# Cross-attention's output projection in one fixed order with sums grown from the seventh product's, tiles transposed in pairs, and the norm row on partition 96

## Chip, cores and metric

The kernel runs on one core of one Trainium2 chip. The metric is the device time of one execution in microseconds; the median of three runs of the kernel before is 856.6 us (856.55 to 857.37).

## The reference

One layer of an encoder on a residual stream x of 512 tokens by 1024 columns, in float32: a token mixer (HGRN2 and mLSTM heads in both directions), a cross-attention to 256 memory tokens in four heads of 256 columns, and a squared-ReLU MLP of width 4096, each behind an RMSNorm, and a last RMSNorm. The change touches the norm at the start and this part:

```python
def cross_attention(xn, memn, w_q, w_kv, w_o):
    q = (xn @ w_q).reshape(b, s, XATTN_HEADS, XATTN_HEAD_DIM)
    k, v = jnp.split(memn @ w_kv, 2, axis=-1)
    scores = jnp.einsum('bqhd,bkhd->bhqk', q, k).astype(jnp.float32) * (XATTN_HEAD_DIM ** -0.5)
    p = jax.nn.softmax(scores, axis=-1).astype(v.dtype)
    o = jnp.einsum('bhqk,bkhd->bqhd', p, v).reshape(b, s, D_MODEL)
    return o @ w_o

x = x + cross_attention(rmsnorm(x, norm_xattn[l]), rmsnorm(mem, norm_mem[l]), ...)
x = x + squared_relu_mlp(rmsnorm(x, norm_mlp[l]), w_up[l], w_down[l])
```

## The kernel before

**Number format and weights.** Every float32 operand is split in a high part (ScalarE, a copy to fp32r, line 254) and a low part (VectorE, a subtraction, line 255); a product is three matmuls, high by high, high by low, low by high (`mm3`, lines 258 to 260). The weights come in 512 KB blocks of 128 x 1024 in the order of use through SP's queue into three buffers (`load`, line 233); the split parts have three buffers each (`wh`, `wl`), so a block's split waits until TensorE has used the block three places ahead of it. `split` and `weights` make these splits ahead of their use, under high priority.

**Order of instructions.** A scheduler orders each engine's instructions by priority and program order and by what it thinks is ready; every engine then runs its own list strictly in order. In a `manual_schedule` block the listed engines keep program order. Before, TensorE's is the program's order in the first norm and from the loop over the four MLP blocks on, and the scheduler's in between. `behind(a, b)` ties a behind b on their engine.

**Start.** Six small matmuls on a tile of ones keep TensorE running (line 157). The norm's gain row is fetched into row 0 of a tile that VectorE has set to zero (lines 148 and 149, two halves), and a matmul by ones spreads it over all partitions (`spread`, line 161). For each of four token tiles: a sum of squares on ScalarE (`x_stat`, line 327), a power on GpSimd (line 196), scaling on VectorE (`x_scale`, line 332), four transposes (line 337), the split, and the first projection's products. The constants, with the identity for the transposes, come by ScalarE's queue (line 150).

**Cross-attention.** For each head the query projection (`proj_d`) is followed by a chain in three parts that `tick` advances one at a time: scores, softmax and scaling (lines 960 to 970); transposes (line 977) and their split; the product with the values and the sums and differences that the next step takes (lines 1011 to 1013). The chain of head 3 is still open when the output projection begins.

**Output projection.** `by_blocks` does it by a scheme of seven products, P1 to P7, of half-size blocks instead of eight. Each product has two halves g; each half has 24/2 = 12 matmuls of 512 columns for two token tiles u. `JOBS[-1]` gives the order P1, P7, P2, P5, P6, P3, P4. P1, P2 and P3 take plain weight blocks; the others take sums of blocks that are built by GpSimd's accumulating DMAs (line 1053): `sum_loads` loads T3 = (0,1)+(1,1) for P7 and U = (0,1)+(0,0) for P5 during the query projections. When P5's split has read U, block (1,1) is added to it for P6, and when P6's split has read that, (1,0) for P4. `ahead` makes the splits of three jobs under high priority. `finished` adds a product to the residual tiles `xr` (`add_out`, line 1169) once or twice. With a tile's last addition its sum of squares follows (line 906), and, some products later (`turn_whole`), its four transposes (`transp`, line 920), each of whose 128-column blocks ScalarE and VectorE split (lines 925 and 926) into x3T, the MLP's input. The tiles of the last product, P4, are transposed inside `first_two`, which runs the first two products of the MLP and then the transposes of the row of norms (line 1197). GpSimd then starts building the MLP's own sums.

Of the kernel before, what the change touches and what calls it, by code (L numbers as in the profile page):

```python
# [10 lines left out]
F32 = mybir.dt.float32  # L11
# [7 lines left out]
P = 128  # L19
# [61 lines left out]
def trunk(ctx: ExitStack, tc: tile.TileContext, x, mem, wpk, vec, cst, lmask, rmask, rows, out):  # L81
# [55 lines left out]
    def behind(a, b):  # L137

        tc.add_manual_dep(a.ins, b.ins.name, mybir.DependencyInfo(mybir.DependencyClass.NoSync, mybir.DependencyReason.DATA),
                          reason="order of an engine")  # L140

    def load_x(t):
        nc.sync.dma_start(out=xtile[t], in_=x[t * P:t * P + P, :])

    load_x(0)
    for g in range(2):
        z = slice(g * 512, g * 512 + 512)
        v.memset(grow1[:, z], 0.0)
        behind(nh_made, nc.scalar.dma_start(out=grow1[0:1, z], in_=rows[0:1, z]))
    nc.scalar.dma_start(out=cs, in_=cst[:, 0:NC1])  # L150
    gmix = [smb(), smb()]
    idle = mmb()

    def keep_busy(n):

        for _ in range(n):
            pe.matmul(idle[:, 0:P], lhsT=ones[:, 0:P], rhs=ones[:, 0:P], start=True, stop=True)

    def spread(g):

        pe.matmul(gmix[g], lhsT=ones[:, 0:P], rhs=grow1[:, g * 512:g * 512 + 512], start=True, stop=True)

    with tc.manual_schedule(engines={mybir.EngineType.PE}):
        keep_busy(6)
        spread(0)
        keep_busy(3)

    def small_setup():
        lmf = A4()
# [66 lines left out]
    def split(i):  # L236
        if i >= NSTREAM or i in hl_tiles:
            return
        load(i)
        s = st_tiles[i]  # L240
        hi, lo = T("wh", 1024, 3, F32R), T("wl", 1024, 3, F32R)
        split_out(hi, lo, s)
        hl_tiles[i] = (hi, lo)

    def weights(key):
        i = SIDX[key]
# [5 lines left out]

    def split_out(dst_hi, dst_lo, src):
        sc.activation(dst_hi, src, AF.Copy)  # L254
        v.tensor_tensor(out=dst_lo, in0=src, in1=dst_hi.bitcast(F32), op=ALU.subtract)  # L255

    def mm3(ps, ah, al, bh, bl, first, last):
        pe.matmul(ps, lhsT=ah, rhs=bh, start=first, stop=False)  # L258
# [66 lines left out]
    def x_stat(t):  # L325
        ss = tiny(1)
        sc.activation(junk, xtile[t], AF.Square, accum_out=ss)
        rx[t], _ = rstd_of(ss, 1, D)
# [26 lines left out]
    with tc.high_priority(), tc.manual_schedule(engines={ET.PE, ET.DVE, ET.Activation}):  # L355
        x_stat(0)
        x_scale(0, 0)
        x_turn(0, 0)
        spread(1)
        split(0)  # L360
        x_stat(1)
        x_split(0, 0)
        part_v(0, 0)
        x_scale(1, 0)
        x_turn(1, 0)
        split(1)
# [524 lines left out]
    xr = {}  # L891
# [142 lines left out]
    def block(f, g, kh, c):  # L1034
        return SIDX["t", "down" if f >= 0 else "xo", max(f, 0) * 8 + 2 * g + 4 * kh, 512 * c]
# [15 lines left out]
    def add_block(dst, idx, accumulate=True):  # L1051
        kw = dict(accum_op=ALU.add) if accumulate else {}
        return gp.dma_start(out=dst, in_=wpk[idx], **kw)  # L1053

    PLAIN = {"P1": (0, 0), "P2": (1, 0), "P3": (1, 1)}
    SUMS = {f: {"P6": "T2" if f >= 0 else "U", "P5": "U", "P7": "T3", "P4": "T2" if f >= 0 else "U"} for f in range(-1, 4)}

    def job(f, n):

        if n >= len(JOBS[f]):  # L1060
            if f < 3:
                split(SIDX["d", "up", 0, 1024 * (f + 1)] + n - len(JOBS[f]))
            return None
        p, g = JOBS[f][n]
        if p in PLAIN:
# [12 lines left out]
        return jobs_hl[f, n]  # L1078
# [78 lines left out]

    def heads_in(p, g):

        if (p, g) in (("P1", 0), ("P7", 0), ("P7", 1)):  # L1160
            tick()
        while p == "P2" and len(sta_o[2 * g + 1]) < 7:
            tick()
        if (p, g) == ("P5", 0):
            drain()

    def add_out(t, c, ps, sign, last):
        z = xr[t, c]
        v.tensor_tensor(out=z, in0=z, in1=ps, op=ALU.add if sign > 0 else ALU.subtract)
        if last:  # L1170
            stats(st2, t, c)
            whole.append([1 if c else 4, t, c])

    whole = []
# [12 lines left out]
    drain()  # L1187
    x3 = xk(x3T)
# [40 lines left out]

    def first_two():  # L1230

        w = [weights(("d", "up", 0, P * 4 * j)) for j in range(2)]
        two = [mmb(), mmb()]
        transp((x3T, V_MLP), *whole.pop(0)[1:])
        for half in (4, 0):
            for j in range(2):
                for k in range(half, half + 4):
                    z = slice(k * P, k * P + P)
                    mm3(two[j], w[j][0][:, z], w[j][1][:, z], x3[k][0], x3[k][1], k == 4, k == 3)
                    if whole and k == 5:  # L1240
                        transp((x3T, V_MLP), *whole.pop(0)[1:])
        rms_row()
        return two

    ctx.enter_context(tc.manual_schedule(engines={mybir.EngineType.PE}))
    for f in range(4):

        sta = []
# [134 lines left out]
```

## Time and profile before

| | |
|---|---|
| median of three runs | 856.6 us |
| the profiled execution | 856.94 us, its span 855.2 us |
| granted TensorE clock | 0.997 |
| TensorE busy, 0 to 12 us | 9.25 us |
| TensorE busy, 470 to 520 us, in tens of us | 8.76, 10.00, 8.44, 8.83, 8.49 |
| TensorE busy, 540 to 800 us | 60.00 of 60, 100.00 of 100, 100.00 of 100 |
| VectorE busy, 470 to 520 us, in tens of us | 8.07, 9.62, 6.63, 8.82, 9.21 |

The profile records one execution. A row names line, engine, operation and the tile written, with the tiles read behind the arrow; PE is TensorE, PEld its weight loads, DVE VectorE, ACT ScalarE, POOL GpSimd, SP the queue that most loads go through. `L920 ... x4` groups four neighbours in time. Idle time stands in brackets with what ended it. TensorE's ends are modelled, so the distance between two starts is the measure of a matmul.

### The profile page before, as it was taken

Reading aid. Unit: us, or ns where it says so; the run is one execution under the profiler, and the core shown is the slowest. Engines: PE = TensorE matmul, PEld = TensorE weight load, DVE = VectorE, ACT = ScalarE, POOL = GpSimd, SP = SyncE. Lnnn points to the kernel's source line nnn. Section 1 sums busy time; section 2 is a strip of 40 time slices with the busy share of each in tenths; the row PEclk is TensorE's granted clock in tenths of the full one; section 3 lists DMA queues with packets and bytes.
Section 4 is the critical chain, followed back from the end, with each engine's and each line's share of the span. In section 5 each row is a group of like instructions: output and inputs, shape, how many; then the busy total and the mean of one; then the engine's idle time right before and its main releaser. Section 6 shows DMA issues by size and latency. Waiting matters only on the chain.

```text
span 855.2 us, 11759 instructions
## 1 busy us (share of the span) xinstructions
PE 836.6 (98%) x4432; PEld 689.5 (81%) x4432; DVE 591.0 (69%) x1042; ACT 437.0 (51%) x795; POOL 76.8 (9%) x126
## 2 busy tenths in 40 slices
PE   8999999999999999999999989999999999999995
PEld 6788888887977987887888767888888888888884
DVE  5568874599368977555567886776667656866675
ACT  5246454444578485454455475553454334435544
POOL 1000000100010000100000004103101210221001
PEclk9999999999999999999999999999999999999998
DMA  7332223122242332542251357969935992698332
GB/s 267 115 130 80 69 81 136 42 98 78 71 128 73 109 130 91 180 108 98 75 149 50 83 115 242 265 166 236 287 109 126 272 265 99 169 277 217 114 60 99
DMA packets 34124, 118.86 MB, mean 139 GB/s; under 512 B 3922, under 2 KB 4050, under 8 KB 34068
## 3 DMA queue, kind: packets, MB, share of 16 engines
q1 hardware_dynamic: 22832, 77.80, 26.5%
q0 software_dynamic: 10944, 39.85, 21.0%
q8 instruction: 35, 0.57, 0.3%
q10 hardware_dynamic: 292, 0.47, 0.2%
q14 instruction: 21, 0.17, 0.1%
HBM read 116.00 MB, written 2.10 MB: 138 GB/s over the span
## 4 chain that ended last, share of the span: by engine, by line
PE 86%; issue 6%; DVE 3%; DMA 2%; ACT 2%; POOL 1%; POOLq 0%; ACTq 0%; DVEq 0%
PE mm L258 18%; PE mm L260 18%; PE mm L259 18%; PE sm L1100 5%; PE sm L1102 5%; PE sm L1101 5%; PE sm L473 2%; PE sm L777 2%; PE sm L762 2%; PE sm L543 2%; PE mm L1102 1%; PE mm L1100 1%; PE mm L1101 1%; DVE wl L255 1%; ACT wh L254 1%
## 5 line engine op out<-in xcount | busy, mean ns | idle before, releaser
L254 ACT ACTIVATE wh<-st 128x1024 fp32r<-128x1024 f32 x131 | 138.6, 1060 | 187.8 <-PE mm L259 119.1
L255 DVE TENSOR_TENSOR wl<-st,wh 128x1024 fp32r<-128x1024 f32 x131 | 160.2, 1224 | 85.4 <-ACT wh L254 84.5
L258 PE MATMUL mm<-xT,wh 128*128 128x512 f32 x544 | 216.2, 398 | 0.0
L259 PE MATMUL mm<-xT,wh 128*128 128x512 f32 x544 | 213.0, 391 | 0.5 <-DVE xT L926 0.5
L260 PE MATMUL mm<-xT,wl 128*128 128x512 f32 x544 | 212.7, 391 | 0.1
L259 PEld LDWEIGHTS mm<-xT,wh 128*128 128x128 f32 x544 | 102.3, 188 | 22.5 <-DVE xT L926 1.6
L258 PEld LDWEIGHTS mm<-xT,wh 128*128 128x128 f32 x544 | 102.2, 188 | 21.9 <-issue 0.7
L260 PEld LDWEIGHTS mm<-xT,wl 128*128 128x128 f32 x544 | 102.1, 188 | 21.9 <-DVE wl L255 0.3
L1053 POOL DMA_DIRECT2D as<-in_wpk x56 | 43.1, 772 | 313.7 <-DVE wl L255 221.6
L1262 DVE SCALAR_TENSOR_TENSOR t<-mm,rg 128x512 f32<-128x512 f32 x32 | 22.0, 691 | 52.2 <-PE mm L260 52.1
L254 ACT ACTIVATE wh<-as 128x1024 fp32r<-128x1024 f32 x30 | 31.9, 1062 | 42.2 <-PE sm L1102 24.8
L1100 PE MATMUL sm<-wh,yT 128*128 128x512 f32 x128 | 49.8, 389 | 0.0
L1101 PE MATMUL sm<-wl,yT 128*128 128x512 f32 x128 | 49.8, 389 | 0.0
L1102 PE MATMUL sm<-wh,yT 128*128 128x512 f32 x128 | 49.8, 389 | 0.0
L255 DVE TENSOR_TENSOR wl<-as,wh 128x1024 fp32r<-128x1024 f32 x30 | 36.8, 1225 | 17.6 <-ACT wh L254 17.4
L196 POOL TENSOR_TENSOR tiny<-tiny,misc 128x4 f32<-128x4 f32 (+1 forms) x14 | 11.9, 848 | 280.6 <-DVE tiny L194 280.6
L1101 PE MATMUL sm<-wl,a 128*128 128x512 f32 x84 | 33.0, 393 | 0.0
L1100 PE MATMUL sm<-wh,a 128*128 128x512 f32 x84 | 32.8, 391 | 0.0
L1102 PE MATMUL sm<-wh,a 128*128 128x512 f32 x84 | 32.8, 390 | 0.0
L1215 DVE TENSOR_TENSOR vv<-vv,sm 128x512 f32<-128x512 f32 x48 | 31.0, 680 | 1.2 <-PE sm L1102 1.2
L1102 PEld LDWEIGHTS sm<-wh,yT 128*128 128x128 f32 x128 | 24.0, 188 | 5.0
L1101 PEld LDWEIGHTS sm<-wl,yT 128*128 128x128 f32 x128 | 24.0, 188 | 5.0
(305 smaller groups left out, 1584.0 us busy)
## 6 DMA issues: line engine op xcount, KB each, us to landing
st<-in_wpk SPq DMA_DIRECT2D x131, 512.0 KB, 3.3
as<-in_wpk POOLq DMA_DIRECT2D x56, 512.0 KB, 6.6
gate<-in_wpk POOLq DMA_DIRECT2D x20, 512.0 KB, 8.0
as<-in_x SPq DMA_DIRECT2D x4, 512.0 KB, 6.1
vv<-in_x SPq DMA_DIRECT2D x8, 256.0 KB, 3.9
out<-vv SPq DMA_DIRECT2D x7, 256.0 KB, 2.2
a<-in_mem SPq DMA_DIRECT2D x2, 512.0 KB, 4.0
t<-in_rows SPq DMA_DIRECT2D x2, 256.0 KB, 3.6
```

Source lines behind the costliest of these rows:

```text
L254: sc.activation(dst_hi, src, AF.Copy)
L255: v.tensor_tensor(out=dst_lo, in0=src, in1=dst_hi.bitcast(F32), op=ALU.subtract)
L258: pe.matmul(ps, lhsT=ah, rhs=bh, start=first, stop=False)
L259: pe.matmul(ps, lhsT=ah, rhs=bl, start=False, stop=False)
L260: pe.matmul(ps, lhsT=al, rhs=bh, start=False, stop=last)
L473: mm = pe.matmul(ps[64 * i:64 * i + 64, z:z + 64], lhsT=kc[j][:, w * P + 64 * i:w * P + 64 * i + 64], rhs=rhs(j, w * P, i), start=True, st ...
L1053: return gp.dma_start(out=dst, in_=wpk[idx], **kw)
L1100: pe.matmul(ps, lhsT=ah, rhs=bh, start=new, stop=False, **fl)
L1101: pe.matmul(ps, lhsT=ah, rhs=bl, start=False, stop=False, **fl)
L1102: pe.matmul(ps, lhsT=al, rhs=bh, start=False, stop=end and k == 1, **fl)
L1215: v.tensor_tensor(out=z, in0=z, in1=ps, op=ALU.add if sign > 0 else ALU.subtract)
L1262: v.scalar_tensor_tensor(out=y, in0=ps, scalar=0.0, in1=rrow[:, 0:512], op0=ALU.max, op1=ALU.mult)
```

## The change

1. The norm's gain row goes to partition 96 of its tile in one transfer, issued first on ScalarE's queue, with the constants tied behind it; only rows 0 to 95 are set to zero, and the spreading matmul contracts 97 rows. One more small matmul stands behind the first spread. The split of the first transposed tile stands ahead of the second tile's sum of squares.
2. P6's sum is grown from P7's: block (0,0) is added to T3 once P7's split has read it; (1,0) follows for P4 as before.
3. TensorE keeps program order from the output projection on, and the three open parts of head 3's chain stand behind P1's first half, P7's first half and P7's second half.
4. Tiles are transposed in pairs (two token tiles, four column blocks in two PSUM tiles) with 256-column splits, once the second tile of a pair has its last addition.
5. `first_two` runs its matmuls on the finished half of the columns, then the last pair, then the rest; the third MLP weight's split is tied behind the last addition.

```diff
+    row_load = nc.scalar.dma_start(out=grow1[96:97, :], in_=rows[0:1, :])
     load_x(0)
+    behind(nc.scalar.dma_start(out=cs, in_=cst[:, 0:NC1]), row_load)
     for g in range(2):
-        z = slice(g * 512, g * 512 + 512)
-        v.memset(grow1[:, z], 0.0)
-        behind(nh_made, nc.scalar.dma_start(out=grow1[0:1, z], in_=rows[0:1, z]))
-    nc.scalar.dma_start(out=cs, in_=cst[:, 0:NC1])
+        v.memset(grow1[0:96, g * 512:g * 512 + 512], 0.0)
...
-        pe.matmul(gmix[g], lhsT=ones[:, 0:P], rhs=grow1[:, g * 512:g * 512 + 512], start=True, stop=True)
+        pe.matmul(gmix[g], lhsT=ones[0:97, 0:P], rhs=grow1[0:97, g * 512:g * 512 + 512], start=True, stop=True)
...
-        keep_busy(3)
+        keep_busy(4)
...
+        x_split(0, 0)
         x_stat(1)
-        x_split(0, 0)
...
-    SUMS = {f: {"P6": "T2" if f >= 0 else "U", "P5": "U", "P7": "T3", "P4": "T2" if f >= 0 else "U"} for f in range(-1, 4)}
+    SUMS = {f: {"P6": "T2", "P5": "U", "P7": "T3", "P4": "T2"} for f in range(4)}
+    SUMS[-1] = {"P6": "T3", "P5": "U", "P7": "T3", "P4": "T3"}
...
-            if f < 0 and p == "P5":
-                add_block(s_, block(f, g, 1, 1))
+            if f < 0 and p == "P7":
+                add_block(s_, block(f, g, 0, 0))
...
-        if (p, g) in (("P1", 0), ("P7", 0), ("P7", 1)):
+        if (p, g) in (("P1", 1), ("P7", 1), ("P2", 0)):
             tick()
...
-            whole.append([1 if c else 4, t, c])
+            if t % 2:
+                whole.append([1 if c else 4, t - 1, c])
...
+    def turn_two(t, c):
+        for k0 in (0, 2):
+            ps = smb()
+            for k in range(2):
+                for u in range(2):
+                    pe.transpose(ps[:, k * 256 + u * P:k * 256 + u * P + P], xr[t + u, c][:, (k0 + k) * P:(k0 + k) * P + P], ident)
+            for k in range(2):
+                kk, z = k0 + k, ps[:, k * 256:k * 256 + 256]
+                g = vc[:, V_MLP + 4 * c + kk:V_MLP + 4 * c + kk + 1]
+                hi = x3T[c][:, kk * 1024 + t * P:kk * 1024 + t * P + 256]
+                lo = x3T[c][:, kk * 1024 + 512 + t * P:kk * 1024 + 512 + t * P + 256]
+                sc.activation(hi, z, AF.Copy, scale=g)
+                v.scalar_tensor_tensor(out=lo, in0=z, scalar=g, in1=hi.bitcast(F32), op0=ALU.mult, op1=ALU.subtract)
...
-                transp((x3T, V_MLP), w[1], w[2])
+                turn_two(w[1], w[2])
...
+    ctx.enter_context(tc.manual_schedule(engines={mybir.EngineType.PE}))
     by_blocks(-1, sta_o, (mm2, mm2, sm2, sm2), add_out, heads_in, turn_whole)
...
-        w = [weights(("d", "up", 0, P * 4 * j)) for j in range(2)]
+        i0 = SIDX["d", "up", 0, 0]
+        for j in range(2):
+            split(i0 + j)
+        w = [hl_tiles[i0 + j] for j in range(2)]
+        for j in range(2, 5):
+            load(i0 + j)
         two = [mmb(), mmb()]
-        transp((x3T, V_MLP), *whole.pop(0)[1:])
...
-                    if whole and k == 5:
-                        transp((x3T, V_MLP), *whole.pop(0)[1:])
+                    if whole and j == 0 and k == 7:
+                        turn_two(*whole.pop(0)[1:])
+                        with tc.high_priority():
+                            behind(split(i0 + 2), last_add[0])
```

More of the change, by code (lines that the diff above doesn't have):

```diff
@@ L241, in split @@
         hi, lo = T("wh", 1024, 3, F32R), T("wl", 1024, 3, F32R)
-        split_out(hi, lo, s)
+        made = split_out(hi, lo, s)
         hl_tiles[i] = (hi, lo)
+        return made
     def weights(key):
@@ L254, in split_out @@
         sc.activation(dst_hi, src, AF.Copy)
-        v.tensor_tensor(out=dst_lo, in0=src, in1=dst_hi.bitcast(F32), op=ALU.subtract)
+        return v.tensor_tensor(out=dst_lo, in0=src, in1=dst_hi.bitcast(F32), op=ALU.subtract)
     def mm3(ps, ah, al, bh, bl, first, last):
@@ L1168, in add_out @@
         z = xr[t, c]
-        v.tensor_tensor(out=z, in0=z, in1=ps, op=ALU.add if sign > 0 else ALU.subtract)
+        last_add[0] = v.tensor_tensor(out=z, in0=z, in1=ps, op=ALU.add if sign > 0 else ALU.subtract)
         if last:
             stats(st2, t, c)
-            whole.append([1 if c else 4, t, c])
-    whole = []
+            if t % 2:
+                whole.append([1 if c else 4, t - 1, c])
+    whole, last_add = [], [None]
+    def turn_two(t, c):
[11 more added lines that the diff above has]
+                v.scalar_tensor_tensor(out=lo, in0=z, scalar=g, in1=hi.bitcast(F32), op0=ALU.mult, op1=ALU.subtract)
     def turn_whole(now=False):
@@ L1239, in first_two @@
                     mm3(two[j], w[j][0][:, z], w[j][1][:, z], x3[k][0], x3[k][1], k == 4, k == 3)
-                    if whole and k == 5:
-                        transp((x3T, V_MLP), *whole.pop(0)[1:])
+                    if whole and j == 0 and k == 7:
+                        turn_two(*whole.pop(0)[1:])
+                        with tc.high_priority():
+                            behind(split(i0 + 2), last_add[0])
         rms_row()
         return two
-    ctx.enter_context(tc.manual_schedule(engines={mybir.EngineType.PE}))
     for f in range(4):
```

## The prediction

> **What bounds the kernel now.** I read the page first, then the busy time by stretches, the waits of the stage that the diff touches, its instructions in order of time, and last the first 12 us.
>
> ```profile
> span 855.2 us, 11759 instructions
> ...
> PE 836.6 (98%) x4432; PEld 689.5 (81%) x4432; DVE 591.0 (69%) x1042; ACT 437.0 (51%) x795; POOL 76.8 (9%) x126
> ```
>
> TensorE is the bound: it lacks 18.6 us of the span. What can be won is either one of those idle stretches or an instruction that TensorE does too much. The stretches (start:end, length, then busy time of PE, PEld, DVE, ACT, POOL) tell where they lie:
>
> ```profile
> 0.00:12.00 12.00, 9.25 (x31) 6.77 (x32) 4.58 (x9) 6.98 (x10) 1.64 (x9) 1.00 0.85 326
> 12.00:30.00 18.00, 18.00 (x93) 14.44 (x92) 12.64 (x19) 8.52 (x14) 2.62 (x9) 1.00 0.37 130
> 540.00:600.00 60.00, 60.00 (x266) 49.71 (x265) 42.49 (x58) 26.98 (x33) 9.39 (x13) 1.00 0.86 218
> ```
>
> ```profile
> 463.70:530.00 66.30, 60.80 (x294) 48.97 (x293) 51.43 (x99) 39.01 (x83) 9.81 (x14) 1.00 0.45 122
> ```
>
> The last row is the stage of the diff: the last head's scores, the output projection by seven products, its transposes, and the first two products of the MLP. PE is idle for 5.5 us of it, DVE is busy for 51.4 of 66.3 us. Behind it PE is gapless (60.00 of 60), so what this stage saves arrives at the end in full. The waits of that stage (who <- for whom: total, times, longest):
>
> ```profile
> PE sm L920 <- DVE vv L1169: 4.0, 3, 1.6
> ...
> ACT wh L254 <- DMA as<-in_wpk: 6.2, 2, 4.8
> ...
> PE sm L977 <- DVE t L970: 1.2, 1, 1.2
> ```
>
> So 4.0 us are three times the transposes of the new residual (L920) waiting for its last addition (L1169). Why additions are late, DVE and POOL show:
>
> ```profile
> 493.69 1.23 DVE L255 TENSOR_TENSOR wl<-as,wh 128x1024 fp32r<-128x1024 f32 x1 [3.31 <-ACT wh L254]
> 494.83 1.28 DVE L1169 TENSOR_TENSOR vv<-vv,mm 128x512 f32<-128x512 f32 x2
> ...
> 517.80 1.22 DVE L255 TENSOR_TENSOR wl<-st,wh 128x1024 fp32r<-128x1024 f32 x1
> ...
> 519.20 0.68 DVE L1169 TENSOR_TENSOR vv<-vv,mm 128x512 f32<-128x512 f32 x1
> ```
>
> ```profile
> 485.82 0.86 POOL L1053 DMA_DIRECT2D as<-in_wpk  x1 [53.23 <-DVE wl L255]
> ```
>
> ```profile
> 488.54 6.43 DMA as<-in_wpk
> ```
>
> P6's weight sum is P5's plus one block, added by a DMA that can start only when P5's split has read the sum (485.8, 488.5); it takes 6.4 us. ACT and DVE are already queued on its split, DVE sits idle for 3.31 us, and P2's additions, whose products are done, stand behind it. At 517.8 the same happens with a split of MLP weights ahead of the last addition.
>
> **The change, part by part.** First, what TensorE must do in that stage in any case.
>
> ```profile
> 463.72 0.28 PE L258 MATMUL sm<-a,yT 128*128 128x256 f32 x1
> ...
> 464.31 0.28 PE L260 MATMUL sm<-a,yT 128*128 128x256 f32 x1
> ...
> 475.66 0.60 PE L977 MATMUL sm<-cs,t 128*128 128x128 f32 x4
> ...
> 491.12 0.39 PE L1100 MATMUL sm<-wh,xT 128*128 128x512 f32 x1
> ...
> 493.61 0.39 PE L1102 MATMUL sm<-wh,xT 128*128 128x512 f32 x1
> ...
> 508.17 0.60 PE L920 MATMUL sm<-cs,vv 128*128 128x128 f32 x4
> 508.53 0.47 PE L1101 MATMUL sm<-wl,a 128*128 128x512 f32 x1
> 508.84 0.39 PE L1102 MATMUL sm<-wh,a 128*128 128x512 f32 x1
> ...
> 519.93 0.66 PE L920 MATMUL sm<-cs,vv 128*128 128x128 f32 x4 [1.26 <-DVE vv L1169]
> ...
> 530.00 0.60 PE L1197 MATMUL sm<-cs,tiny 128*128 128x128 f32 x4
> ```
>
> The stage runs from the first score (463.72) to the transposes behind the first two MLP products (530.00), 66.3 us. Steps between starts: eleven of a 512-column matmul from 491.12 to 493.61, 0.226 us; five of a 256-column one in 0.59 us, 0.118; four transposes take 0.36 us, 0.09 each, and the matmul behind them lasts 0.31 instead of 0.226 to the next start, so a group costs 0.085 on top. By the code there are 168 matmuls of seven products, 12 for the last head's values and 48 of the MLP: 228 x 0.226 = 51.6; 24 scores x 0.118 = 2.8; 8 + 32 transposes x 0.09 = 3.6; five groups with the pairs x 0.085 = 0.4. Sum 58.4 us: 7.9 us are to be had, idle time, restarts and five spared groups.
>
> *Sums grown from P7's.* T3 is loaded ahead as before; block (0,0) is added behind P7's split instead of (1,1) behind P5's. Both additions go out from POOL some 20 us earlier and are needed for P6, over 24 us later, against 6.4 us of transfer. The number of issues is the same (two and two, 0.86 us each on POOL, which was idle for 53 us before them). P4's addition follows P6's split; it has the rest of P6 and all of P3, some 36 matmuls or 8.2 us, against 6.4. This removes the 3.31 us in which DVE stood still, and the first two L920 waits. The cover is gone if P6's splits slip by 1.7 us; each us more is then lost.
>
> *The fixed PE order.* The ticks move: scores of head 3 stand behind P1's first half, its transposes behind P7's first half, its values behind P7's second. PE now waits in order where the scheduler had filled in with P1's matmuls. The first such place is the scores, which need the low part of the last query block:
>
> ```profile
> 464.78 1.23 DVE L255 TENSOR_TENSOR wl<-gate,wh 128x1024 fp32r<-128x1024 f32 x1 [0.18 <-ACT wh L254]
> ...
> 467.19 0.68 DVE L255 TENSOR_TENSOR yT<-mm,yT 128x512 fp32r<-128x512 f32 x1
> ```
>
> It is there at 467.87. P1's first half (12 x 0.226 = 2.7 us from 463.72) ends at 466.4, and five scores later, at 467.0, PE stands: 0.9 us, with all of PE queued behind it. The remaining scores then end near 470.2. The transposes follow 24 matmuls (5.4 us) later, at 475.6; now, where the scores end at the same time, the softmax let the second half of them start at 475.66: 0 to 0.5 us. The values have 2.7 us of cover for the two splits of the transposed weights: nothing, unless a weight split goes first (1.06 us on ACT, by the first 128x1024 activation quoted below, and 1.23 on DVE).
>
> *Pairs.* L925 and L926 fall from 32 to 16 instructions each, 256 columns instead of 128:
>
> ```profile
> L926 DVE SCALAR_TENSOR_TENSOR xT<-sm,vc,xT 128x128 fp32r<-128x128 f32 x32 | 9.9, 345 | 1.3 <-ACT xT L925 1.2
> ...
> L255 DVE TENSOR_TENSOR a<-t,a 128x256 fp32r<-128x256 f32 x4 | 1.7, 418 | 0.0
> ```
>
> Taking 0.42 us for a 256-column one, DVE saves 9.9 - 16 x 0.42 = 3.2 us and is left with 48.2 us of work in a stage of 58.4: 83% busy, so it is not the bound, but has queues. A pair waits for both additions; the last pair stands behind 12 matmuls (2.7 us) of the MLP and the additions take 0.68 us, so that wait (1.26 of the 4.0, at 519.93) goes, as the split that stood ahead of the addition is now tied behind it. That tie delays the third MLP weight's low part, needed 36 matmuls (8.2 us) later: nothing.
>
> Residual waits at the hand-offs that I can't follow I bound by 0 and by the two splits that could stand in the way at two of them, 2 x (1.06 + 1.23) = 4.6 us; nearest to rows that show cover, I take 0.9. Stage: 7.9 - 0.9 - 0.9 = 6.1 us gained; bounds 3.4 (4.6 of waits, the 0.9 avoided) and 7.9.
>
> *The start.*
>
> ```profile
> cs<-in_cst ACTq DMA_DIRECT2D x1, 196.0 KB, 4.3
> ```
>
> ```profile
> 0.74 0.41 ACTq L150 DMA_DIRECT2D cs<-in_cst  x1
> ```
>
> ```profile
> 1.44 4.11 DMA rg<-in_rows
> ...
> 5.68 2.04 PE sm L161 x2
> 7.72 1.28 PE mm L157 x6
> 9.00 0.82 PE sm L337 x4
> ```
>
> ```profile
> 4.87 1.06 ACT L327 ACTIVATE gate<-as 128x1024 f32<-128x1024 f32 x1 [1.13 <-DMA as<-in_x]
> ...
> 6.29 0.56 POOL L196 TENSOR_TENSOR tiny<-tiny,misc 128x1 f32<-128x1 f32 x1 [5.22 <-DVE tiny L194]
> ...
> 7.82 0.75 DVE L332 SCALAR_TENSOR_TENSOR as<-as,tiny,sm 128x512 f32<-128x512 f32 x1 [1.62 <-PE sm L161]
> ...
> 9.86 0.60 ACT L254 ACTIVATE xT<-sm 128x512 fp32r<-128x512 f32 x1 [1.07 <-PE sm L337]
> ...
> 11.75 1.22 DVE L255 TENSOR_TENSOR wl<-st,wh 128x1024 fp32r<-128x1024 f32 x1
> ```
>
> The norm row waited for the memset; on partition 96 it goes out at about 0.74, first in ACT's queue. If it lands by 3.9, the 2.04 us spread ends by 6.0 and four warming products (4 x 1.28/3 = 1.7) by 7.7; the scale can start at 6.9, when the first row's power is there (6.85), and end at 7.65. So transposes start at 7.7 instead of 9.0. But the first split now stands ahead of the second statistics on ACT: transposes to 8.5, split 0.60, statistics to power 1.98 (4.87 to 6.85), scale 0.75: the second weight's low part starts at 11.8, where it starts now at 11.75. The 1.3 us are given back: 0.0, bounds +0.5 (x first in the DMA engines, since the constants go out later) and -1.2 (the row lands at 5.0, 4.3 us after issue like the 196 KB of constants do now; spread and warming then hold the transposes to 8.8). The constants, delayed by 0.4 us, are needed at 7.7. The memsets of 96 rows lie under the row's transfer.
>
> The Trainium skill, DMA: Bandwidth & Descriptors, section Queues, rings and completion order, speaks against: a transfer's semaphore is written only after all earlier writes of that DMA engine, over all its queues. By it the row could be told no sooner than the first x tile behind whose packets it lies, and the sum would be 1.2 us worse; no run here shows yet how a row that goes first fares.
>
> Sum: 856.94 us (the profiled execution) - 6.1 - 0.0 = 850.8 us. The median of the runs shown is 0.34 us lower than that execution, so 850.5 us for the median.
>
> **The rivals.**
> *The queue on DVE decides* (0.25): DVE at 83% with splits ahead of additions keeps waits of 4.6 us beside the scores' 0.9: 7.9 - 5.5 = 2.4, 854.1 us. For it: all PE waits quoted end on DVE. Against: the longest came from a DMA in front of it, which is gone.
> *The row is held back* (0.12): it lands with the first x tile at about 5.0, the start loses 1.2 us: 851.7. For it: it took 4.11 us in before; against: it stood behind 196 KB of its own queue then. This is what the Trainium skill's rule above would make of the start.
> *Slower* (0.04): at each hand-off in fixed order (scores, transposes, values, P2 and P5 of head 3, four pairs: nine) one weight split of 1.06 + 1.23 = 2.29 us goes first with no cover. Five of nine cost 11.5 us, more than the 7.9: 860.2 us; from four (9.2) it is slower. Against: every hand-off has 12 matmuls or more, 2.7 us, as cover.
> *The change doesn't do what it says* (0.06): the grown sum lands late or the lead is lost later, as where up-weights and sums share the DMA engines: 856.3. Against: 60.00 us of 60 busy at a DMA share of 0.86.
>
> **How the numbers follow.** The forecast as worked out has 0.53. Likeliest time 850.5; the range takes in the DVE rival and the upper bound of the gain in part: 848.6 to 854.4. 0.2% is 1.7 us, about what can be told from no change here: faster by more holds the forecast, the row and most of the DVE case, 0.89; within it 0.07; slower 0.04.
>
> **What would show it.** Right: no ACT wait for a weight sum by DMA in the stage, none or one L920 wait under 1 us, 16 of L925 and L926 at about 0.42 us, the stage 60 us long, a short wait of the scores on the yT split, the row's landing before 4 us, and the second weight split still near 11.8. Wrong: L920 or L977 waits of over 1 us, a DVE over 90% busy between, a transfer on the chain of the stage, a span above 853.

## The result and the profile after

The changed kernel takes 851.64 us (median of six runs, 851.56 to 851.79), the kernel before 856.58 (six runs, 855.86 to 857.37): a ratio of 0.9942, interval 0.9929 to 0.9954, or 4.9 us less. 850.5 was forecast, 848.6 to 854.4 the range. One run of the kernel before, beside e9 to e12 below, took 2535.74 us and stands in no range here. The profiled execution of the changed kernel took 851.79 us. Its page, first the span, then busy time of each engine:

```profile
span 850.0 us, 11734 instructions
...
PE 834.7 (98%) x4434; PEld 689.3 (81%) x4434; DVE 589.4 (69%) x1026; ACT 434.1 (51%) x779; POOL 76.6 (9%) x126
```

The busy time by stretches (start:end, length, then PE, PEld, DVE, ACT, POOL), for the stage of the diff and for a part behind it:

```profile
463.48:524.72 61.24, 59.67 (x294) 49.69 (x293) 49.41 (x83) 36.39 (x67) 8.59 (x13) 1.00 0.48 127
540.00:594.00 54.00, 54.00 (x240) 44.72 (x239) 38.88 (x52) 24.44 (x30) 8.51 (x12) 1.00 0.86 218
```

The stage is 61.24 us long where it was 66.28 (463.72 to 530.00), with the same 294 matmul records; it begins 0.24 us earlier (here with P1's first matmul, as the scores now stand behind P1's first half). 5.04 and 0.24 make up the 5.2 us by which the span is shorter (rounding aside), and TensorE still has no gap behind it, so the gain arrives whole. TensorE's waits over the whole span (total, times, longest):

```profile
PE sm L337 <- DVE as L332: 2.0, 2, 1.3
...
PE sm L1184 <- DVE vv L1170: 0.8, 1, 0.8
PE sm L260 <- DVE yT L255: 0.7, 1, 0.7
```

The second and third row are all that is left in the stage: a pair's transposes that wait for an addition, and the scores that wait for the query's low part. VectorE around the first of them, in order of time:

```profile
499.35 1.28 DVE L1170 TENSOR_TENSOR vv<-vv,mm 128x512 f32<-128x512 f32 x2
500.54 1.22 DVE L255 TENSOR_TENSOR wl<-gate,wh 128x1024 fp32r<-128x1024 f32 x1
501.68 1.28 DVE L1170 TENSOR_TENSOR vv<-vv,mm 128x512 f32<-128x512 f32 x2
```

No additions wait for a weight sum any more; one weight split of 1.22 us went ahead of two additions whose products were done. GpSimd's issues of the sums, and ScalarE's largest wait in the stage, show what became of the transfers:

```profile
466.07 0.86 POOL L1053 DMA_DIRECT2D gate<-in_wpk  x1 [33.52 <-DVE wl L255]
469.07 0.85 POOL L1053 DMA_DIRECT2D gate<-in_wpk  x1 [2.14 <-DVE wl L255]
490.44 0.86 POOL L1053 DMA_DIRECT2D gate<-in_wpk  x1 [20.52 <-DVE wl L255]
493.79 0.85 POOL L1053 DMA_DIRECT2D gate<-in_wpk  x1 [2.49 <-DVE wl L255]
```

```profile
ACT wh L254 <- PE mm L259: 5.8, 3, 3.8
```

The first two are P6's additions, 20 us earlier than the 485.82 of before; P6's splits begin at 487.59 and 490.31, over 21 us behind them. The last two are P4's, whose splits begin at 499.44 and 502.16, 9.0 and 8.4 us behind them. From issue to landing these transfers took 5.3 to 5.4 us. ScalarE (window 463 to 525) now waits for TensorE to free split buffers; the 6.2 us for a DMA's sum are gone from the stage. The splits of the transposed tiles, by groups (busy, mean ns of one):

```profile
L1191 DVE SCALAR_TENSOR_TENSOR xT<-sm,vc,xT 128x256 fp32r<-128x256 f32 x16 | 7.4, 480 | 1.4 <-ACT xT L1190 1.3
L1190 ACT ACTIVATE xT<-sm,vc 128x256 fp32r<-128x256 f32 x16 | 7.1, 469 | 3.0 <-PE sm L1184 2.3 <-DVE xT L1191 0.6
```

And the start, in order of time:

```profile
0.74 0.54 ACTq L145 DMA_DIRECT2D rg<-in_rows  x1
...
3.72 1.55 PE L160 MATMUL sm<-rg,t 97*128 97x512 f32 x2
...
4.63 1.06 ACT L327 ACTIVATE gate<-as 128x1024 f32<-128x1024 f32 x1 [1.81 <-DMA as<-in_x]
...
7.43 0.66 PE L337 MATMUL sm<-cs,as 128*128 128x128 f32 x4 [1.27 <-DVE as L332]
...
8.12 0.60 ACT L254 ACTIVATE xT<-sm 128x512 fp32r<-128x512 f32 x1 [0.97 <-PE sm L337]
8.62 1.05 ACT L327 ACTIVATE gate<-as 128x1024 f32<-128x1024 f32 x1
...
11.28 1.22 DVE L255 TENSOR_TENSOR wl<-st,wh 128x1024 fp32r<-128x1024 f32 x1
```

TensorE spreads the row (L160) without a wait for it. In the kernel before the first transposes stood here:

```profile
8.79 1.03 PE L337 MATMUL sm<-cs,as 128*128 128x128 f32 x4
```

(The prediction's 9.00 is the same group as the chain that ended last has it.) So they begin at 7.43 instead of 8.79, the second tile's statistics at 8.62 instead of 7.64, and the second weight's low part at 11.28 instead of 11.75.

### The profile page after: what moved, and what is told of

It is laid out like the page before. It is cut to its first block, busy times and chain, and to the rows that moved or that the text cites. A ratio compares the mean times of both kernels' runs of the same rounds, so it can differ in the third digit from the quotient of the medians.

```text
span 850.0 us, 11734 instructions
## 1 busy us (share of the span) xinstructions
PE 834.7 (98%) x4434; PEld 689.3 (81%) x4434; DVE 589.4 (69%) x1026; ACT 434.1 (51%) x779; POOL 76.6 (9%) x126
## 4 chain that ended last, share of the span: by engine, by line
PE 87%; issue 6%; DVE 3%; ACT 2%; DMA 1%; POOL 1%; POOLq 0%; ACTq 0%; DVEq 0%
PE mm L258 18%; PE mm L259 18%; PE mm L260 18%; PE sm L1101 5%; PE sm L1103 5%; PE sm L1102 5%; PE sm L473 2%; PE sm L777 2%; PE sm L543 2%; PE mm L1103 1%; PE mm L1101 1%; PE mm L1102 1%; PE sm L762 1%; ACT wh L254 1%; DVE wl L255 1%
## 5 line engine op out<-in xcount | busy, mean ns | idle before, releaser
L1053 POOL DMA_DIRECT2D as<-in_wpk x52 | 39.6, 763 | 249.5 <-DVE wl L255 161.3
L254 ACT ACTIVATE wh<-as 128x1024 fp32r<-128x1024 f32 x26 | 27.6, 1062 | 37.0 <-PE sm L1103 23.7
L255 DVE TENSOR_TENSOR wl<-as,wh 128x1024 fp32r<-128x1024 f32 x26 | 31.9, 1226 | 14.0 <-ACT wh L254 13.9
L195 POOL TENSOR_TENSOR tiny<-tiny,misc 128x4 f32<-128x4 f32 (+1 forms) x14 | 11.8, 845 | 280.2 <-DVE tiny L193 280.2
```

The lines of the kernel that those rows point to most:

```text
L255: return v.tensor_tensor(out=dst_lo, in0=src, in1=dst_hi.bitcast(F32), op=ALU.subtract)
```

## The experiments

The theory: the sums' transfers cost the old stage its largest idle time, the wide splits keep VectorE's queue short enough for the fixed order, and the order and the start give nothing by themselves. Rivals: the gain is the fixed order's; or it is the start's; or VectorE's queue decides. All times are medians; the kernel before, on the same chips, took 856.25 to 856.5 us. The changed kernel was not timed again beside them, so a difference of less than 0.4 us from its median needs the stage lengths to back it. "Stage" is that of each kernel's profiled execution.

| kernel | us | range of its runs | ratio to before, interval | stage |
|---|---|---|---|---|
| the changed kernel | 851.64 | 851.56 to 851.79 | 0.9942, 0.9929 to 0.9954 | 61.24 |
| e1 sums alone, on before | 853.40 | 852.63 to 853.96 | 0.9968, 0.9954 to 0.9982 | 63.00 |
| e2 sums undone | 853.79 | 852.65 to 854.74 | 0.9971, 0.9959 to 0.9982 | 64.16 |
| e3 order undone | 851.32 | 851.23 to 851.34 | 0.9941, 0.9926 to 0.9956 | 60.89 |
| e4 pairs undone | 856.81 | 855.94 to 857.00 | 1.0004, 0.9995 to 1.0013 | 66.59 |
| e5 statistics first | 850.97 | 850.84 to 851.46 | 0.9938, 0.9925 to 0.9950 | 61.26 |
| e6 constants first | 853.29 | 851.99 to 853.62 | 0.9961, 0.9947 to 0.9975 | 61.25 |
| e7 query split first | 850.69 | 850.63 to 851.31 | 0.9935, 0.9922 to 0.9949 | 60.27 |
| e8 pair later | 850.57 | 850.50 to 850.59 | 0.9932, 0.9919 to 0.9944 | 60.16 |
| e9 = e5 + e7 + e8 | 849.01 | 848.98 to 849.09 | 0.9912, 0.9897 to 0.9926 | 59.19 |
| e10 = e4, wait filled | 855.33 | 855.11 to 855.72 | 0.9987, 0.9978 to 0.9996 | 64.98 |
| e11 = e4, pair later | 854.69 | 854.61 to 856.52 | 0.9984, 0.9975 to 0.9993 | 64.32 |
| e12 start undone | 851.64 | 850.58 to 852.21 | 0.9940, 0.9927 to 0.9954 | 61.19 |

**e1, the sums alone.** The kernel before with part 2 of the change alone:

```diff
-    SUMS = {f: {"P6": "T2" if f >= 0 else "U", "P5": "U", "P7": "T3", "P4": "T2" if f >= 0 else "U"} for f in range(-1, 4)}
+    SUMS = {f: {"P6": "T2", "P5": "U", "P7": "T3", "P4": "T2"} for f in range(4)}
+    SUMS[-1] = {"P6": "T3", "P5": "U", "P7": "T3", "P4": "T3"}
...
-            if f < 0 and p == "P5":
-                add_block(s_, block(f, g, 1, 1))
+            if f < 0 and p == "P7":
+                add_block(s_, block(f, g, 0, 0))
```

> The kernel before with the one change of the sums: P6's sum grown from P7's, everything else as before. Theory (VectorE stood still for 3.31 us on a split that waited for an accumulating transfer, with P2's additions behind it): the two waits of the transposes of 1.56 and 1.17 us go, with their restarts about 3 us less than 856.6, so 853.4 to 855.0. Rival (the fixed order of TensorE is what brings the gain, the sums only move): within 0.5 us of 856.6.

The median falls by 3.1 us, and the stage by 3.28, from 66.28. Of TensorE's waits in it these are left:

```profile
PE sm L920 <- DVE vv L1170: 1.3, 1, 1.3
PE sm L977 <- DVE t L970: 1.2, 1, 1.2
```

Two of the three waits at L920 are gone with the 3.31 us in which VectorE had stood still: the sums are most of the gain, and need no other part of the change. The other 1.8 us of the stage come with parts 3 to 5: TensorE's waits there are 2.8 us in e1 (the 0.3 us for a low part counted) and 1.57 in the changed kernel, and five groups of transposes are spared. Part 5 was not undone by itself.

**e2, the sums undone**, the other parts kept: the same lines in reverse, on the changed kernel.

> The changed kernel with the sums as before (P5's sum grown for P6). Theory that the sums bring most of the gain: 3 us over 851.6, about 854.6, with the wait of ScalarE on the accumulating transfer back at over 3 us. Rival: in the fixed order P5's split is read some 3 to 4 us earlier against P6 than before (480.5 and 485.9 against P6 at 492.8), so a transfer of 6.4 us is there at 488.4 and 493.8 and the loss is 0 to 1 us, 851.6 to 852.6.

2.15 us more by the medians, 2.92 by the stage, between the two forecasts. ScalarE's wait for the sum is back, 0.95 us for P6's first split and 3.05 for the second (at 492.70). TensorE waits 1.94 us for the addition ahead of the second pair, and behind that wait the granted clock (the number behind POOL's count) falls to half:

```profile
504.17 0.98 PE L1183 MATMUL sm<-cs,vv 128*128 128x128 f32 x7 [1.94 <-DVE vv L1169]
```

```profile
506.00:507.00 1.00, 1.00 (x4) 0.78 (x3) 0.67 (x2) 0.69 (x2) 0.00 (x0) 0.50 0.00 0
```

The six runs fall in two groups: 852.65 to 853.06 us, with a mean granted clock of 0.996 to 0.998 over the run, and 854.53 to 854.74, each with 0.994; the profile is of the upper group. By these clocks, undoing the sums costs 1.0 to 1.4 us where the clock holds and 2.9 to 3.1 where it falls. e4 and e10 below take up the clock.

**e3, the order undone.** TensorE's order in the projection is the scheduler's again, and the three steps of head 3 stand where they stood:

```diff
-        if (p, g) in (("P1", 1), ("P7", 1), ("P2", 0)):
+        if (p, g) in (("P1", 0), ("P7", 0), ("P7", 1)):
...
-    ctx.enter_context(tc.manual_schedule(engines={mybir.EngineType.PE}))
     by_blocks(-1, sta_o, (mm2, mm2, sm2, sm2), add_out, heads_in, turn_whole)
...
+    ctx.enter_context(tc.manual_schedule(engines={mybir.EngineType.PE}))
     for f in range(4):
```

> The changed kernel with TensorE's order in the output projection left to the scheduler again and the three open parts of head 3 where they stood. Theory: the 0.75 us wait of the scores goes, the wait of the transposed softmax weights (1.2 us before) comes back, and transposes of the residual are placed by the scheduler: 852 to 853.5. Rival (the order brings most): over 854.

0.3 us less, not more, and below both forecasts; the stage is 0.35 us shorter too. The scheduler's order pays one wait of 1.2 us, L977 for the softmax, and not the two that the fixed order pays (0.75 and 0.82 us). The fixed order is not where the gain comes from.

**e4, the pairs undone.** Each pair is turned at the same place, as two single tiles with 128-column splits:

```diff
-                turn_two(w[1], w[2])
+                for u in range(2):
+                    transp((x3T, V_MLP), w[1] + u, w[2])
...
```

(and the same for the last pair in `first_two`).

> The changed kernel with each pair turned as two single tiles at the same place: 32 splits of 128 columns on ScalarE and VectorE instead of 16 of 256. Theory (VectorE is not the bound, queues are short): 0.3 to 1.0 us over 851.6, from some 3 us more work on VectorE in a stage of 61 us. Rival (VectorE's queue decides): 2 us or more over it, with waits on splits or additions of over 2 us.

All of the gain is lost: 856.81 us, far above the 0.3 to 1.0 us that the theory allowed, and the rival holds. TensorE, in order of time:

```profile
501.69 0.60 PE L920 MATMUL sm<-cs,vv 128*128 128x128 f32 x4
504.91 0.72 PE L920 MATMUL sm<-cs,vv 128*128 128x128 f32 x4 [2.61 <-DVE vv L1170]
...
506.28 0.63 PE L1103 MATMUL sm<-wh,a 128*128 128x512 f32 x1
506.71 0.63 PE L1101 MATMUL sm<-wh,a 128*128 128x512 f32 x1
```

The wait that the changed kernel has at this pair with 0.82 us is 2.61 us. VectorE says why:

```profile
502.10 0.68 DVE L1170 TENSOR_TENSOR vv<-vv,mm 128x512 f32<-128x512 f32 x1
503.03 1.23 DVE L255 TENSOR_TENSOR wl<-gate,wh 128x1024 fp32r<-128x1024 f32 x1 [0.25 <-ACT wh L254]
504.17 0.68 DVE L1170 TENSOR_TENSOR vv<-vv,mm 128x512 f32<-128x512 f32 x1
```

With eight splits of 346 ns for a pair instead of four of 480, its list is in another order, and a second weight split, which follows the additions in the changed kernel, stands ahead of the last one. And the matmuls behind the wait start 0.43 us apart, not 0.23. The granted clock in the stretches there:

```profile
504.00:505.00 1.00, 0.09 (x1) 0.10 (x2) 1.00 (x3) 0.12 (x1) 0.00 (x0) 1.00 0.00 0
505.00:506.00 1.00, 1.00 (x6) 0.91 (x7) 0.22 (x2) 1.00 (x4) 0.00 (x0) 0.68 0.00 0
506.00:507.00 1.00, 1.00 (x4) 0.81 (x3) 0.82 (x3) 0.75 (x3) 0.00 (x0) 0.50 0.00 0
507.00:508.00 1.00, 1.00 (x4) 0.72 (x4) 0.03 (x1) 0.37 (x1) 0.00 (x0) 0.50 0.00 0
508.00:509.00 1.00, 1.00 (x4) 0.84 (x3) 0.77 (x2) 0.04 (x1) 0.00 (x0) 0.61 0.00 0
```

What is missing to 1.00 in the last four rows adds up to 1.71 us: so much TensorE time the low clock takes on top of the wait. Nine of the ten runs took 856.66 to 857.00 us with a mean clock of 0.995 or 0.996; the tenth took 855.94 with 0.997.

The narrow splits cost this much only in the fixed order. e1 has them in the scheduler's order and takes 853.40 us; e3, wide splits in that order, with the new start and the new `first_two` besides, takes 851.32. There they and what goes with them are worth 2.1 us, here 5.2.

**e10, the wait filled.** e4 with ten products of the identity by itself ahead of the transposes that waited; the transposes overwrite what they write, so they add work and change no output:

```diff
+        for _ in range(fill):
+            pe.matmul(ps[:, 0:P], lhsT=ident, rhs=ident, start=True, stop=True)
         for k in range(4):
             pe.transpose(ps[:, k * P:k * P + P], xr[t, c][:, k * P:k * P + P], ident)
...
+                    transp((x3T, V_MLP), w[1] + u, w[2], 10 if (w[1], w[2], u) == (2, 1, 1) else 0)
```

> The kernel with the pairs turned as singles (856.81 us), with ten extra 128x128 products of the identity in TensorE's order ahead of the four transposes that waited 2.61 us at 504.9 us; they write a PSUM tile that the transposes then overwrite, and change no output. Theory: it is the idle time of TensorE that brought the granted clock to 0.50 for some 3.4 us and cost about 1.7 us there; with the array at work through the wait the clock stays at 1.00, the projection's matmuls after it stay at 0.39 us in the rows instead of 0.63, and the time is 854.9 to 855.4 us. If the ten products take longer than the wait, what they take over is added. Rival: the clock falls for another reason than the idle time, or its fall is covered by work that waits for VectorE anyway: the time stays at 856.5 to 857.0 us.

TensorE's rows at the same place (this kernel has two lines more above, so L922 is e4's L920 and its L920 the filling; the trace holds each of the ten products as two records):

```profile
502.12 0.60 PE L922 MATMUL sm<-cs,vv 128*128 128x128 f32 x4
502.67 2.50 PE L920 MATMUL sm<-cs 128*128 128x128 f32 x20
505.34 0.66 PE L922 MATMUL sm<-cs,vv 128*128 128x128 f32 x4 [0.17 <-DVE vv L1172]
...
506.29 0.40 PE L1105 MATMUL sm<-wh,a 128*128 128x512 f32 x1
506.53 0.39 PE L1103 MATMUL sm<-wh,a 128*128 128x512 f32 x1
```

The second transposes come 3.22 us behind the first (505.34 - 502.12), as in e4 (504.91 - 501.69): the addition is no sooner there. But the array was at work, and the matmuls behind are 0.23 us apart again. Granted clock:

```profile
506.00:507.00 1.00, 1.00 (x6) 0.78 (x6) 0.61 (x2) 0.84 (x5) 0.00 (x0) 1.00 0.00 0
507.00:508.00 1.00, 1.00 (x6) 0.84 (x5) 0.89 (x2) 0.71 (x3) 0.00 (x0) 1.00 0.00 0
```

855.33 us, 1.48 less than e4, for ten products that compute nothing. All ten runs (855.11 to 855.72, mean clock 0.996 to 0.998) lie below all of e4's. So at this place it was the idle time that brought the clock down.

**e11, singles turned later.** e4 with the second pair one product later (the edit of e8).

> The kernel with the pairs turned as singles (856.81 us), with the pair of blocks 2 and 3 of the upper half turned one product later. Theory: most of what the narrow splits cost is the one wait of 2.61 us and the low clock behind it (about 1.7 us). With 2.7 us more of TensorE work ahead of these transposes that wait falls under 1 us, the clock stays, and the time is 852.5 to 853.6 us; what is left over the changed kernel (0.9 to 2.0 us) is VectorE's longer work at the stage's end (the first wait of the MLP, 1.3 us). Rival: VectorE's longer queue sets the stage, and the wait only moves to the last pair or to the MLP's first product: 855.5 us or more.

854.69, between the two forecasts. The pair stands six matmuls or 1.36 us later, not 2.7 as the expectation has it, and the wait at L920 falls by about that, from 2.61 to 1.26 us. In the profiled execution the clock stays at 1.00 (two of the ten runs, 856.15 and 856.52 us, have mean clocks of 0.995 and 0.994, the others, 854.61 to 854.76, 0.996 or 0.997). But the queue moved part of the wait on:

```profile
PE mm L259 <- DVE xT L926: 2.2, 3, 1.3
PE sm L920 <- DVE vv L1170: 1.3, 1, 1.3
```

The first products of the MLP now wait 0.70 us at 514.98 and 1.28 at 517.23 for the low parts. With the scores' 0.75, TensorE waits 3.99 us in the stage against 1.57 in the changed kernel: 2.4 of the 3.1 us between the two. So of the 5.2 us that e4 loses, 1.5 go with the low clock (e10); turning the pair later gives back 2.1, the clock and part of the wait; 3.1 stay at this later place too, 2.4 of them waits for VectorE.

**e8, the pair later**, with the wide splits: the pair of tiles 2 and 3 of the second half of the columns is turned one product later.

```diff
-                whole.append([1 if c else 4, t - 1, c])
+                whole.append([4 if not c else 2 if t == 3 else 1, t - 1, c])
```

> The changed kernel with the second pair (token tiles 2 and 3, second half of the columns) turned one product of six matmuls, 1.36 us, later. Theory: the wait of 0.82 us (1.05 with the restart) for P6's last additions goes: 850.5 to 850.8. Rival (VectorE's queue is what is late, so the wait comes back at the next pair or at the first MLP matmuls): 851.3 to 852.

**e7, the query split first**: head 3's query split under high priority.

```diff
-            split_out(d[:, 0:512], d[:, 512:1024], ps)
+            with (tc.high_priority() if h == 3 else ExitStack()):
+                split_out(d[:, 0:512], d[:, 512:1024], ps)
```

> The changed kernel with the split of head 3's query blocks under high priority: VectorE then does its low part before three smaller operations of head 2. Theory: the scores' wait of 0.75 us, 1.0 with the restart, goes, and nothing else moves: 850.6 to 850.9. Rival (the operations of head 2 that it overtakes come late in turn, or the softmax is pushed behind a split): no gain, 851.5 to 852.5.

e8 takes the pair's wait away, for 1.07 us, and e7 the scores', for 0.95, as forecast. Each costs some 0.2 us over its idle time. At the scores, the last matmul ahead of the wait is counted with its full 0.28 us, not the 0.12 between two starts, and the first behind it has 0.23 to the next start.

**e5, the statistics first**: the second tile's sum of squares stands ahead of the first split again, the rest of the new start kept.

```diff
-        x_split(0, 0)
         x_stat(1)
+        x_split(0, 0)
```

> The changed kernel with the second tile's sum of squares ahead of the first transposed tile's split again, the row still on partition 96. Theory (the early row's 1.3 us are given back because the split stands in front of the second statistics on ScalarE): the second weight's low part starts near 10.6 instead of 11.28, the start is 0.5 to 0.7 us shorter and the kernel 851.0 to 851.3, if nothing behind it clips the lead. Rival (the lead is clipped behind the start anyway, as 0.47 us at 12.5 became 0.24 at 463): 851.5 to 851.7.

0.67 us less: that is what the swapped order gives back of the earlier row. The profiled execution is the longest of the five, 851.46 us, and there the second weight's low part starts at 11.00, not at 10.6: the transposes meet the constants, which stand behind the row on their queue:

```profile
7.93 0.63 PE L337 MATMUL sm<-cs,as 128*128 128x128 f32 x4 [0.60 <-DMA cs<-in_cst]
```

**e6, the constants first**: the two loads on ScalarE's queue change places.

```diff
-    row_load = nc.scalar.dma_start(out=grow1[96:97, :], in_=rows[0:1, :])
+    cs_load = nc.scalar.dma_start(out=cs, in_=cst[:, 0:NC1])
     load_x(0)
-    behind(nc.scalar.dma_start(out=cs, in_=cst[:, 0:NC1]), row_load)
+    behind(nc.scalar.dma_start(out=grow1[96:97, :], in_=rows[0:1, :]), cs_load)
```

> The changed kernel with the constants first on ScalarE's queue again and the norm's row behind them (not behind the memset, which stays on rows 0 to 95). If the row of the kernel before was late because of the memset, it lands as early as now, by 3.5 us, and the time stays at 851.6. If it was late because it stood behind the 196 KB of its queue, it lands at 4.5 to 5.6, the spread starts then, the transposes come about 1 us later and the time is 852.0 to 853.0, with more spread from run to run.

```profile
1.25 0.48 ACTq L147 DMA_DIRECT2D rg<-in_rows  x1
...
4.88 1.06 ACT L327 ACTIVATE gate<-as 128x1024 f32<-128x1024 f32 x1 [2.19 <-DMA as<-in_x]
5.25 1.10 PE L160 MATMUL sm<-rg,t 97*128 97x512 f32 x2 [1.32 <-DMA rg<-in_rows]
```

Issued 0.5 us later and behind 196 KB, the row is there at 5.25 and not before 3.72, though it waits for no clearing: its place in the queue is enough to make it about as late as it was in the kernel before. In this execution (851.99 us) that costs the transposes only 0.25 us, 7.68 against 7.43; the other three took 1.2 to 1.6 us more and have no profile, so what they lost is not shown.

**e12, the start undone**: the whole start of the kernel before, the rest changed.

> The changed kernel with the whole start of the kernel before: the row of the latent's mean in two loads of 2 KB to partition 0 behind the clearing of the other partitions, the constants after them, one group fewer of products that keep TensorE awake, and the square's statistics ahead of the first split. Theory: the new start gave the 0.24 us by which the changed kernel's stage began earlier, and more in those executions in which the old start met a low clock: a median of 851.8 to 852.9 us, and a spread from run to run of 1 us or more, as the kernel before has it (855.02 to 857.52), against 0.23 us for the changed kernel. Rival: the start is worth nothing and the spread belongs to the stage: 851.5 to 851.8 us and a spread under 0.4 us.

(What the expectation calls the latent's mean is the norm's gain row.) 851.64, the changed kernel's own median: the start is worth nothing, as far as six runs that spread over 1.63 us can tell. e1's runs, with the old start, spread over 1.33 us, and those of the kernel before over more (855.02 to 857.52, beside e1 to e8); the changed kernel's over 0.23, and those of e3, e5 and e7 to e10, whose row goes first too, over 0.09 to 0.68. Two profiles with the old start show what varies. e12's, and behind it e1's, whose stage began at 462.65, 1.2 us sooner than e12's (463.88):

```profile
5.77 2.05 PE L161 MATMUL sm<-rg,t 128*128 128x512 f32 x2 [1.84 <-DMA rg<-in_rows]
```

```profile
5.76 1.10 PE L161 MATMUL sm<-rg,t 128*128 128x512 f32 x2 [1.83 <-DMA rg<-in_rows]
```

The same spreading product (two records in the trace) behind the same wait takes 2.05 us or 1.10, and the transposes begin at 8.89 or 7.77. The column of the granted clock reads 1.00 in both, so why it is the one or the other stays open. The new start spreads the row at 3.72 with 1.27 us of slack ahead of the transposes. In e5's profile the spread and the products behind it end 1.2 us later than in the changed kernel's, and TensorE still stands idle before the transposes.

**e9, all three edits** (e5, e7, e8).

> After with three edits of its order at once, each of which was timed by itself: the square's statistics ahead of the first split of x (alone 0.67 us under the changed kernel), the split of head 3's query ahead in its engines' order (alone 0.95 us), the second pair one product later (alone 1.07 us). Theory: the three waits stand at three places, 8 us, 467 us and 503 us, with full engines between them, so the gains add: 851.64 - 0.67 - 0.95 - 1.07 = 848.95 us, 848.5 to 849.4, and a stage of about 59.2 us, which is its TensorE work without waits. Rival 1: part of the gain at the start is eaten where the chain of splits near 36 us is met, or by the constants' load: 849.4 to 849.9. Rival 2: the stage's two waits are one backlog of VectorE, so that removing both gives no more than removing one: 849.9 to 850.1.

849.01 us, 2.63 under the changed kernel, against a sum of 2.69: the waits stand apart and their gains add. Its stage by stretches has no idle time at all:

```profile
462.85:522.04 59.19, 59.19 (x294) 49.69 (x293) 49.11 (x83) 36.21 (x67) 8.80 (x13) 1.00 0.49 131
```

## Why the prediction was right, and where it was 1.1 us off

- **What bounds it.** Right. TensorE is gapless behind the stage, so 5.04 us of the stage and 0.24 of the start came out as 5.2 of the span.
- **The floor of 58.4 us** was the term mis-sized: e9 has no wait, and takes 59.19. (Its lines stand one lower: L1185 is L1184.) A group of eight transposes lasts longer than the rows of four let me work out:

```profile
492.59 1.04 PE L1185 MATMUL sm<-cs,vv 128*128 128x128 f32 x8
493.38 0.48 PE L1101 MATMUL mm<-wh,a 128*128 128x512 f32 x1
493.70 0.39 PE L1102 MATMUL mm<-wl,a 128*128 128x512 f32 x1
```

  Eight take 0.79 us, not 0.72, so 3.95 for 40 against 3.6; the scores took 2.85 against 2.8; what remains, the matmuls with their restarts, is 52.4 against 51.6 + 0.4: steps of 0.24 us, not 0.226, here and there, not traced further. Together 0.8 us, and it is most of the miss.
- **The sums.** Right, shown by e1: the stage lost 3.28 us, where 3.31 of VectorE's idle time had been named, and no split waits for a sum any more. The cover of P6 held, and that of P4 (8.4 us against 5.3 to 5.4 of transfer).
- **The fixed order.** The scores' wait came where it was put, 0.9 forecast and 0.75 us of idle time at 467.7 measured, for the reason given (e7 removes it). With the restart it cost 1.0. The transposes (0 to 0.5 forecast) and the values cost nothing. But the sum let this part win, by the 1.2 us wait at L977 that it spares against 0.9; e3 shows that it loses 0.3 us, since the pair's wait, too, is absent in the scheduler's order.
- **The residual waits, 0.9.** One wait, 0.82 us, 1.05 with the restart, at one of the hand-offs, from one split ahead of two additions, as the bound had it (e8). The bound, 0 to 4.6, was worked out; the 0.9 inside it was chosen, and that it came this close is luck. 61.24 is e9's 59.19 plus these two, 1.0 and 1.05.
- **Pairs.** 16 and 16 instructions as said, at 0.48 us instead of 0.42 taken. The stage's VectorE work fell by 2.0 us, not 3.2, to 81% of it (49.41 of 61.24). The step put this as relief of an engine that isn't the bound; e4 shows it is a condition of the rest: with narrow splits the rival in which VectorE's queue decides comes true. It comes at 856.81, not 854.1 (by its own terms 854.2): its price left out the low clock, 1.5 us by e10, and stood on the floor that is 0.8 too low.
- **The start.** 0.0 forecast, 0.0 measured by e12, 0.24 in the two profiles. The row landed before 3.72 (by 3.9 forecast); transposes came at 7.43 (7.7), held by the scaling and not by the warming products; the second weight's low part at 11.28 (11.8), since the first tile of x landed 0.24 us sooner and the split and statistics were packed closer than assumed. That the swapped order gives back part of what the earlier row won is shown by e5, at 0.67 us and not 1.3. The transposes came 1.36 us earlier, as forecast, so that the sum still came to 0.0 is in part luck; what took the rest is not traced, and e12's runs spread too far to settle 0.2 us. Not foreseen: the start's gain is in the spread from run to run.
- **The rivals.** The row was not held back by the first tile of x: the spread began at 3.72, statistics of that tile at 4.63. The Trainium skill, DMA: Bandwidth & Descriptors, section Queues, rings and completion order, ties a transfer's semaphore to earlier writes of its DMA engine; the trace agrees as far as it goes, as the row went first on its queue here, and in e6, behind the constants, was told only after that tile (4.88, then 5.25). If the rule holds here, what failed was the rival's premise that the row lies behind x's packets; no view shows the packets' order. A split first at five of nine hand-offs did not happen: it was one.

Sum: 0.8 for the floor and 0.25 for the waits (2.05 against 1.8), less the 0.24 of the start, are 0.8 us. Another 0.2 is that the median stands 0.15 us under its profiled execution, where 0.34 had been taken over from the kernel before, and the last 0.1 is the rest of the span and rounding: 1.1 us.

## What to carry to other kernels

Before a sum is split, ask when its transfer could have started: growing it from an operand that is read two products earlier (P7's instead of P5's) took 3.1 us out of a kernel that was otherwise the same. In TensorE's fixed order both of the waits that were left were paid in full, and the next gain lay in the instruction that stood ahead of what TensorE waited for, or in the place of the wait; three such moves (0.67, 0.95 and 1.07 us) added up to 2.6 us. Price a wait of about 2 us or more at its length and, as a risk, a low clock behind it (1.7 us in e4).

## What the runs showed of the hardware

- In the profiled executions TensorE's clock fell to 0.50 for some 3 us behind idle time of 2.61 us (e4) and 1.94 us (e2), and not behind 1.26 us (e11) or 0.82 (the changed kernel). The length does not settle it alone: runs of one and the same kernel differ, and the longer ones have the lower mean clock (e2 0.994 in three runs of six; e4 0.995 or 0.996 in nine of ten; e11 0.995 and 0.994 in two of ten). The fall in e4 takes 1.71 of some 855 us, which is 0.002 of the mean, so the clock is the likely cause of these groups; the unprofiled runs can't show it. The Trainium skill, TensorE: Matmul & The Clock Gate, section What's actually happening, puts the half clock behind an idle window of about 3.4 us, and its Part 4: PE-mode transpose says that transposes do not count as busy in the same way. Between projection products, transposes included, e4 has 3.63 us (501.69 to 505.32), which agrees, but e2 has 3.19 us (501.72, that is 501.49 and a step of 0.23, to 504.91), less than the page's window, and its clock fell too: here the measurement decides, and in that execution a shorter gap was enough.
- A split of 256 columns takes 480 ns on VectorE and 469 on ScalarE, one of 128 takes 346 and 363: half of the instructions in 65 to 70% of the time.
- A row of 4 KB that went first on its queue was there within 3.0 us (0.74 to 3.72), beside 512 KB tiles on another queue.
